# Forming the sums of an output weight by accumulating DRAM transfers instead of on GpSimd, in a fused fp32 encoder layer

## The chip, the cores and the metric

The kernel runs on one core of one Trainium2 chip, as one program. The metric is the device time of one execution in microseconds (us), the median over several executions. The engines named below are TensorE (PE; PEld is its weight load), VectorE (DVE), ScalarE (ACT), GpSimd (POOL) and SyncE (SP). SP and ACT issue plain transfers; in the changed kernel POOL issues transfers too. All matrix products run in fp32 precision by splitting each operand into a rounded high part and a low rest and adding three products (hi·hi, hi·lo, lo·hi).

## The reference

One layer on x of 1024 tokens by 1024 channels, all float32. What the change touches is the product with `w_out` and what follows it:

```python
h = rmsnorm(x, g_mix)
z = h @ w_in                       # pool channels | q | k | v
y_pool = pool_mixer(z[..., :512], w_pool_grp, pool_scale)
y_attn = diff_attention(q, k, v, ...)      # 8 heads, two softmax maps each
gates = sigmoid(h @ w_gate + b_gate)
merged = gates[..., :1024] * (y_pool @ w_branch_pool) + gates[..., 1024:] * (y_attn @ w_branch_attn)
x = x + merged @ w_out             # w_out is 1024 x 1024
h2 = rmsnorm(x, g_ffn)
x = x + square(relu(h2 @ w_up)) @ w_down
```

## The kernel before

The work stands in four stages, in this order.

1. Start and heads (0 to about 690 us of the span). The eight row tiles x0 to x7 (128 tokens each) are loaded, normalised and transposed into hT: x0 to x3 make the first half of hT, x4 to x7 the second. For each row tile, ACT squares it, DVE and POOL make the scale (`rs4` to `rs7`, or `rsa0` to `rsa2` for the first three; the last step is a power on POOL), DVE scales it (`hn4` to `hn7`), PE transposes it into PSUM (`hps`), ACT and DVE split it into hi and lo parts of hT. Then a pipeline runs over 8 heads times 8 row tiles, one step g per head and tile: projection z on PE (stage A), norm of q and k (stage B: `ms` on DVE and POOL, `qn`), transposes, scores, softmax, weighted sum. The gate projection g (`fillers`, weights `fwgate`, raw loads `frgate`) is put in between as filler for PE. `rqkv` are raw loads of a head's weights, `wqkv` their split forms.
2. Branches (about 690 to 800 us). Products with `w_branch_pool` (into `mp`) and `w_branch_attn` (`ba`), gating, merge. In here stands `w_out_sums`, the code that the change removes.
3. Output product (about 800 to 915 us). `merged @ w_out` is computed by a Strassen-Winograd scheme: seven products of half-size blocks, numbered 1 to 7. The sums of activations are made by DVE from the halves of `mp`; the sums of the four blocks of `w_out` were formed earlier and kept in the DRAM tile `w_sum`, from where `w_set` loads them (tiles `ro`, split into `wo`).
4. The MLP, by the same scheme (915 us to the end).

The order on each engine is set by a scheduler that works through the program with priorities; a program's order of writing is a priority and not a place. An instruction that waits for nothing can therefore be put well ahead of where the code has it. The transfers of SP stand in one queue; so do those of POOL, between its other instructions. The sums of `w_out` before, for each of four row blocks d:

```python
for i, b in enumerate((b1, b2)):
    nc.sync.dma_start(b, w_out[(d + 4 * i) * P : (d + 4 * i + 1) * P, :])
(b11, b12), (b21, b22) = ((b[:, 0:512], b[:, 512:D]) for b in (b1, b2))
sub(pool, b11, b12, b11)
sub(pool, b12, b22, b12)
sub(pool, b22, b22, b11)
sub(pool, b21, b21, b22)
for i, b in enumerate((b1, b2)):
    nc.sync.dma_start(w_sum[i][d * P : (d + 1) * P, :], b)
```

The functions that the diff touches:

Of the kernel before, what the change touches and what calls it, by code (L numbers as in the profile page):

```python
# [8 lines left out]
F32 = mybir.dt.float32  # L9
# [3 lines left out]
ALU = mybir.AluOpType  # L13
# [4 lines left out]
P = 128  # L18
S = 1024
D = 1024  # L20
# [23 lines left out]
N_W1, N_W2 = 9, 16  # L44
POOL_W = (3,)
G_DIST, G_COLS = 3, 2

O = "B1 C2 H7 D4 R8 E5 F6 W-2 A0"
ORDER = [(w[0], int(w[1:])) for w in O.split()]
# [14 lines left out]
def encoder_kernel(  # L64
# [21 lines left out]
    nc = tc.nc  # L86
    x, out = x[0], out[0]
    w_in, w_gate, w_out = w_in[0], w_gate[0], w_out[0]
# [4 lines left out]
    dram = ctx.enter_context(tc.tile_pool(name="dram", bufs=1, space=DRAM))  # L93
# [69 lines left out]
    def fu_tile(name):  # L163
        return fq.tile([P, S], F32, tag="fu", name=name)
# [99 lines left out]
    p_dram = dram.tile([POOLD, S], F32, name="p_dram")  # L264
    g_dram = dram.tile([2 * D, S], F32, name="g_dram")
    yd = dram.tile([S, D], F32, name="yd")

    def rsq(dst, ss, n, c):

        nc.vector.tensor_scalar(dst, ss, c, EPS, op0=ALU.mult, op1=ALU.add)  # L270
        nc.gpsimd.tensor_tensor(dst, dst, mhalf[:, :n], op=ALU.pow)  # L271
# [119 lines left out]
    def gates():  # L391
        for c in range(2 * NK - 2):
            yield from gate_cols(c)
        for gen in [gate_cols(c) for c in (2 * NK - 2, 2 * NK - 1)] * 2:
            next(gen)
            yield

    def fillers():
        gate_units = gates()
        for _ in range(G_FIRST):  # L400
            next(gate_units)
            yield
        for g in range(4):
            for _ in pool_group(g):
                yield
                next(gate_units)
                yield
        for _ in gate_units:
            yield
# [3 lines left out]
    with ExitStack() as ph:  # L413
# [35 lines left out]
        def load_x(t):  # L449
            xs[t] = htile([P, D], F32, f"x{t}", 1) if t < 2 else ut([P, D], F32, f"x{t}")  # L450
            for c in range(0, D, 512 if t < 2 else D):
                e = c + 512 if t < 2 else D
                loads[f"x{t}"] = q(nc.sync.dma_start, xs[t][:, c:e], x[t * P : (t + 1) * P, c:e])
# [25 lines left out]
        def split_w(h, kp, eng):  # L479
            rw = raws.pop((h, kp))  # L480
            for i in range(2):
                w = wt([P, 2, 384], f"wqkv{h}_{2 * kp + i}")
                split(w[:, 0, :], w[:, 1, :], rw[:, i, :], eng)
                Wh.setdefault(h, []).append(w)
# [12 lines left out]
        act, dve, pol = nc.scalar, nc.vector, nc.gpsimd  # L497
# [89 lines left out]
        for j in range(2):  # L587
            gb = ps_z.tile([P, 512], F32, tag="z", name=f"gb{j}")
            for i in range(4):
                k = 4 * j + i  # L590
# [301 lines left out]
        def stage(w, g):  # L892
# [19 lines left out]
            elif w == "W" and t == 0 and h:  # L912
                for kp in range(NK // 2):
                    load_w(h, kp)
                    split_w(h, kp, nc.gpsimd)

        units, made = fillers(), 0
        for g in range(-2, N + 10):
            for t in range(4, NT):
                if LX[t] == g:  # L920
                    load_x(t)
            for t in range(1, NT):
                if NX[t] == g:
                    with tc.issue_after(h_hi[t - 2].ins) if t < 6 else nullcontext():
                        norm_x(t)
            if g == G_DIST:
                with behind():
                    distances()
            if g == G_COLS:
                columns()  # L930
            gens = {}
            for tok in ORDER:
                if tok not in gens:
                    i = g - tok[1]
                    gens[tok] = stage(tok[0], i) if 0 <= i < N else iter(())
                next(gens[tok], None)
            for gen in gens.values():
                for _ in gen:
                    pass
            while made < F_UNITS and made < (g - F_FROM) * F_PACE:  # L940
                next(units)
                made += 1
# [4 lines left out]
    def add(eng, out_, a, b):  # L947
        eng.tensor_tensor(out_, a, b, op=ALU.add)

    def sub(eng, out_, a, b):  # L950
        eng.tensor_tensor(out_, a, b, op=ALU.subtract)

    dve, pool = nc.vector, nc.gpsimd

# [4 lines left out]
    def vt(shape, dt, name):  # L959
        return vpool.tile(shape, dt, tag="V", name=name)  # L960
# [22 lines left out]
    ws_bp = {0: load_cols2(w_branch_pool, 0, "bp0")}  # L983
    ypT = [load_split(p_dram, g * P, f"ypT{g}", ypt_tile) for g in range(4)]
    mp, yT, ws_ba = [], [], {}
    w_sum = [dram.tile([S // 2, D], F32, name=f"w_sum{i}") for i in range(2)]

    def w_out_sums(d):

        b1, b2 = (vt([P, D], F32, f"wos{d}_{i}") for i in range(2))  # L990
        for i, b in enumerate((b1, b2)):
            nc.sync.dma_start(b, w_out[(d + 4 * i) * P : (d + 4 * i + 1) * P, :])
        (b11, b12), (b21, b22) = ((b[:, 0:512], b[:, 512:D]) for b in (b1, b2))
        sub(pool, b11, b12, b11)
        sub(pool, b12, b22, b12)
        sub(pool, b22, b22, b11)
        sub(pool, b21, b21, b22)
        for i, b in enumerate((b1, b2)):
            nc.sync.dma_start(w_sum[i][d * P : (d + 1) * P, :], b)

    for d in range(NK):
        if d % 2 == 0 and d + 2 < NK:
            ws_bp[d + 2] = load_cols2(w_branch_pool, (d + 2) * P, f"bp{d + 2}")
        elif d > NK - 4:
            j = len(ws_ba)
            ws_ba[j] = load_cols(w_branch_attn, j * P, f"ba{j}")
        branch_pool(d, ws_bp[d - d % 2][d % 2], bank)
        if d < 4:
            w_out_sums(d)
        if d % 4 < 2:  # L1010
            rb = [fu_tile(f"rb{d}") if d % 2 else ut([P, S], F32, f"rb{d}")]
        else:
            rb = [tmp(f"rb{d}_{i}") for i in range(2)]
        yT.append(load_split(y_dram, d * P, f"yT{d}", yt_tile(d), (rb, r_dram[d])))
    def half(d, th):
        return mp[d][:, th * 512 : (th + 1) * 512]
# [8 lines left out]
    for d in range(NK):  # L1025
        if d + 2 < NK:
            ws_ba[d + 2] = load_cols(w_branch_attn, (d + 2) * P, f"ba{d + 2}")
        ws = ws_ba.pop(d)
        gp = [tmp(f"gp{d}_{th}") for th in range(2)]
        gate([(gp[0], 0, 512), (gp[1], 512, S)], d)  # L1030
        for th in range(2):
            nc.vector.tensor_tensor(half(d, th), half(d, th), gp[th], op=ALU.mult)
        ga = fu_tile(f"ga{d}") if d % 2 else ut([P, S], F32, f"ga{d}")
        gate(whole(ga)[0], NK + d)
        for th in range(2):
            hs = slice(th * 512, (th + 1) * 512)
            ps = proj_T(bank(f"ba{d}_{th}"), ws, lambda k, th: pair(yT[k][th]), th)
            mg = tmp(f"mg{d}_{th}")
            nc.vector.tensor_tensor(mg, ps, ga[:, hs], op=ALU.mult)
            add(pool, half(d, th), mg, half(d, th))  # L1040
            if th == 0:
                a_set("1" if d < 4 else "2", d % 4)
        if d >= 4:
            e = d - 4
            add(dve, half(e, 1), half(e, 1), half(d, 1))
            sub(dve, half(e, 0), half(e, 1), half(e, 0))
            sub(dve, half(d, 0), half(d, 0), half(e, 0))

# [25 lines left out]
    y = {}  # L1076
# [99 lines left out]
    X = [o_bank(f"oX{t}", t) for t in range(4)]  # L1176
# [13 lines left out]
    ws["5"] = w_set("5")  # L1190
    for d in range(4):
        a_set("5", d)
        sub(dve, half(d, 1), half(d + 4, 1), half(d, 0))

    def keep_sum(t, dh):
        k = half(t + 4 * dh, 0)
        xr = tmp(f"xr{t}_{dh}")
        x_rows(xr, 4 + t, dh)
        add(dve, k, X[t], xr)

    for t in range(4):
        o_product(X[t], "6", t, ws["6"])
# [10 lines left out]
    ws["4"] = w_set("4")  # L1213
    for t in range(4):
        o_product(X[t], "3", t, ws["3"])
        add(dve, y[t][:, 512:D], X[t], y[t][:, 512:D])
        nc.sync.dma_start(yd[t * P : (t + 1) * P, :], y[t])
        square(t, 1, y[t][:, 512:D], tmp(f"nsq1_{t}"))
        norm_scale(t, [y[t][:, 0:512], y[t][:, 512:D]])
    Y = {}  # L1220
    for step in O_TAIL.split():
        t = int(step[1])
        if step[0] == "7":
            Y[t] = pb.tile([P, 512], F32, tag="b", name=f"oZ{t}")
            o_product(Y[t], "7", t, ws["7"])
            k = half(t + 4, 0)
            add(dve, k, Y[t], k)
            y_done(k, 4 + t, 1)
            square(4 + t, 1, k, tmp(f"nsq1_{4 + t}"))
        elif step[0] == "a":  # L1230
            for d in range(4):
                a_set("4", d)
        elif step[0] == "n":
            first_half(t)
        elif step[0] == "s":
            second_scale(4 + t)
        elif step[0] == "t":
            second_turn(4 + t, norm_turn(4 + t, lambda j, name: o_bank(name, 2 * (t % 2) + j)))
        else:
            o_product(Y[t], "4", t, ws["4"])  # L1240
            k = half(t, 0)
            add(dve, k, Y[t], k)
            y_done(k, 4 + t, 0)
# [257 lines left out]
    b11 = {}  # L1501
# [117 lines left out]
```

## Time and profile before

| | |
|---|---|
| time, median of 3 executions | 1529.79 us (1528.99 to 1529.82) |
| profiled execution, first to last instruction (span) | 1526.9 us |
| what lies around the span, median less span | 2.9 us |
| PE busy | 1517.4 us of the span |
| DVE, ACT, POOL busy | 1025.5, 794.6, 389.4 us |
| bytes moved by the DMA engines | 213.75 MB, mean 140 GB/s |

The profiled execution's own time is not listed apart from the runs; it is taken as its span and the 2.9 us around it. How to read the views: a row of a group of instructions has line, engine, operation, tiles, count, busy time and mean duration; a row of a wait has who waited, for whom, the total, the number of waits and the longest; a row of a window has its start and end, its length, the busy time of each engine with the count of instructions, the granted TensorE clock, the share of time in which the DMA engines were busy (1.0 is all 16) and the rate. Matmul records can overlap and their ends are modelled, so PE busy says that PE was not waiting, not that it ran at its best rate. Some matmul records can be missing.

### The profile page before, as it was taken

What the parts mean: (1) busy time and instruction counts of PE and PEld (TensorE: products, weight loads), DVE (VectorE), ACT (ScalarE), POOL (GpSimd) and SP (SyncE); (2) the same over time, 40 slices, a digit from 0 to 9 for tenths busy, and PEclk for the clock granted to TensorE, in tenths of its full rate; (3) what the DMA queues carried; (4) which work ended last, traced back from release to release, by engine and by line L of the source; (5) the groups of instructions that cost most, each with busy time, mean ns of one, the idle gap of its engine ahead of it and who ended that gap; (6) DMA issues with size and microseconds to landing.
All of it is one profiled execution on the core that took longest, in us unless ns stands there. A gap on an engine that the chain in (4) does not pass through costs nothing.

```text
span 1526.9 us, 21743 instructions
## 1 busy us (share of the span) xinstructions
PE 1517.4 (99%) x7637; PEld 1316.2 (86%) x7637; DVE 1025.5 (67%) x2135; ACT 794.6 (52%) x1653; POOL 389.4 (26%) x466
## 2 busy tenths in 40 slices
PE   9999999999999999999999999999999999999999
PEld 8899999999999999888888887888888788888887
DVE  7877766677777777742645899676656678556672
ACT  6655555556555555544633467565555634333331
POOL 5525242434334352318646510000000000000000
PEclk9999999999999999999999999999999999999999
DMA  6212111111202021339745633554433899537650
GB/s 213 66 48 66 34 53 52 59 51 39 73 31 80 33 87 49 118 106 376 269 139 174 212 138 117 173 195 156 152 124 111 290 333 367 182 125 260 229 191 28
DMA packets 168583, 213.75 MB, mean 140 GB/s; under 512 B 10165, under 2 KB 104090, under 8 KB 168474
## 3 DMA queue, kind: packets, MB, share of 16 engines
q1 hardware_dynamic: 151050, 185.05, 36.4%
q10 hardware_dynamic: 17424, 27.31, 4.9%
q8 instruction: 60, 0.98, 0.3%
q14 instruction: 49, 0.40, 0.1%
HBM read 154.62 MB, written 57.70 MB: 139 GB/s over the span
## 4 chain that ended last, share of the span: by engine, by line
PE 96%; DVE 2%; DMA 1%; ACT 1%; issue 0%; SPq 0%; POOLq 0%; POOL 0%; ACTq 0%; DVEq 0%
PE z L138 6%; PE z L139 5%; PE z L140 5%; PE Da L139 4%; PE Da L140 4%; PE Da L138 4%; PE g L138 4%; PE g L139 4%; PE g L140 4%; PE Db L138 3%; PE Db L139 3%; PE Db L140 3%; PE X L138 3%; PE X L139 3%; PE X L140 3%; PE sc L767 2%
## 5 line engine op out<-in xcount | busy, mean ns | idle before, releaser
L138 PE MATMUL z<-wqkv,hT 128*128 128x384 f32 x512 | 173.7, 340 | 1.2 <-ACT hT L131 1.1
L140 PE MATMUL z<-wqkv,hT 128*128 128x384 f32 x512 | 173.6, 339 | 0.4 <-DVE hT L437 0.3
L139 PE MATMUL z<-wqkv,hT 128*128 128x384 f32 x512 | 173.2, 338 | 0.0
L778 ACT ACTIVATE s<-s,nm 128x256 f32<-128x256 f32 (+7 forms) x128 | 99.5, 778 | 77.6 <-DVE nm L770 74.3
L271 POOL TENSOR_TENSOR ms<-ms,mhalf 128x4 f32<-128x4 f32 x64 | 66.7, 1042 | 186.8 <-DVE ms L270 183.3
L138 PE MATMUL g<-hT,fwgate 128*128 128x512 f32 x256 | 101.0, 395 | 0.0
L139 PE MATMUL g<-hT,fwgate 128*128 128x512 f32 x256 | 100.5, 392 | 0.0
L140 PE MATMUL g<-hT,fwgate 128*128 128x512 f32 x256 | 100.4, 393 | 0.0
L138 PEld LDWEIGHTS z<-wqkv,hT 128*128 128x128 f32 x512 | 96.2, 188 | 4.0 <-ACT hT L131 1.2
L140 PEld LDWEIGHTS z<-wqkv,hT 128*128 128x128 f32 x512 | 96.2, 188 | 2.6 <-DVE hT L437 0.9
L139 PEld LDWEIGHTS z<-wqkv,hT 128*128 128x128 f32 x512 | 96.3, 188 | 2.4 <-DVE wqkv L437 0.3
L770 DVE CUSTOM_DVE_ANT_0 s<-sc,dist 128x512 f32<-128x512 f32 (+3 forms) x128 | 74.1, 585 | 21.2 <-PE sc L768 20.3
L767 PE MATMUL sc<-K,Q 128*128 128x512 f32 (+2 forms) x192 | 67.5, 357 | 0.4 <-DVE nm L770 0.4
L768 PE MATMUL sc<-K,Q 128*128 128x512 f32 (+2 forms) x192 | 66.1, 349 | 0.0
L132 DVE TENSOR_TENSOR AS<-s,AS 128x512 fp32r<-128x512 f32 x64 | 43.4, 687 | 30.9 <-ACT AS L131 30.9
L132 POOL TENSOR_TENSOR wqkv<-rqkv,wqkv 128x384 fp32r<-128x384 f32 x56 | 58.7, 1065 | 14.6 <-ACT wqkv L131 14.2
L132 POOL TENSOR_TENSOR fwgate<-frgate,fwgate 128x512 fp32r<-128x512 f32 x32 | 43.5, 1361 | 66.0 <-ACT fwgate L131 66.0
L140 PEld LDWEIGHTS g<-hT,fwgate 128*128 128x128 f32 x256 | 48.1, 188 | 9.5
L138 PEld LDWEIGHTS g<-hT,fwgate 128*128 128x128 f32 x256 | 48.1, 188 | 9.1 <-ACT go L387 0.2
L139 PEld LDWEIGHTS g<-hT,fwgate 128*128 128x128 f32 x256 | 48.1, 188 | 8.8
L132 DVE TENSOR_TENSOR AT_0l<-ta,AT_0h 128x512 fp32r<-128x512 f32 (+1 forms) x48 | 32.0, 666 | 32.0 <-ACT AT_0h L131 31.7
L139 PE MATMUL ba<-yT,wba 128*128 128x512 f32 x128 | 49.6, 389 | 0.0
(481 smaller groups left out, 4625.9 us busy)
## 6 DMA issues: line engine op xcount, KB each, us to landing
wd<-in_w_down_dram SPq DMA_DIRECT2D x56, 512.0 KB, 5.4
wu<-in_w_up_dram SPq DMA_DIRECT2D x32, 512.0 KB, 4.3
udS<-us SPq DMA_DIRECT2D x64, 256.0 KB, 3.3
ur<-udS SPq DMA_DIRECT2D x32, 512.0 KB, 4.5
rqkv<-in_w_in_dram SPq DMA_DIRECT2D x64, 192.0 KB, 3.0
ur<-ud SPq DMA_DIRECT2D x24, 512.0 KB, 6.4
frgate<-in_w_gate_dram SPq DMA_DIRECT2D x32, 256.0 KB, 3.6
g_dram<-go ACTq DMA_DIRECT2D x32, 256.0 KB, 3.2
```

Source lines behind the costliest of these rows:

```text
L132: (lo_eng or nc.vector).tensor_tensor(lo, src, f(hi), op=ALU.subtract)
L138: nc.tensor.matmul(ps, lhs_hi, rhs_hi, start=first, stop=False, **kw)
L139: nc.tensor.matmul(ps, lhs_hi, rhs_lo, start=False, stop=False, **kw)
L140: return nc.tensor.matmul(ps, lhs_lo, rhs_hi, start=False, stop=last, **kw)
L271: nc.gpsimd.tensor_tensor(dst, dst, mhalf[:, :n], op=ALU.pow)
L767: nc.tensor.matmul(dst, Q[:, i, 0, :], rhs, start=True, stop=False)
L768: nc.tensor.matmul(dst, Q[:, i, 1, :], rhs, start=False, stop=True)
L770: nc.vector.tensor_tensor_reduce(out=s[i][:, c : c + w], in0=sc[:, 0:w], in1=dist[:, o0 + c : o0 + c + w], scale=2.0 ** -(h + 1), scalar=B ...
L778: nc.scalar.activation(s[i][:, 0:n], s[i][:, 0:n], AF.Exp, bias=last, scale=-1.0, accum_out=Z[:, i, t : t + 1])
```

## The change

The GpSimd sums of stage 2, with their eight loads and eight stores, go. Instead two DRAM tiles are filled by transfers from DRAM to DRAM: four plain copies of a 512x512 block of `w_out` (1.05 MB each) on SP, and seven accumulating transfers of the same size on POOL, each of which adds a block of `w_out` to what lies in `w_sum`. The code calls them from the loop over g, from g = 12 on in steps of 6. Since a transfer can add but not subtract here, all sums become sums with plus signs, and the minus signs move into the sums of activations (`neg_sub`, which is one DVE instruction with a multiply by -1 and a subtract, in 12 places) and into the additions of the products (`sub` for `add`).

```diff
+SUM_FROM, SUM_STEP = 12, 6
...
+    w_sum = [dram.tile([S // 2, D], F32, name=f"w_sum{i}") for i in range(2)]
...
+        def sum_steps():
+
+            q = {f"{i + 1}{j + 1}": w_out[i * 512 : (i + 1) * 512, j * 512 : (j + 1) * 512] for i in range(2) for j in range(2)}
+            s = {f"T{i}": w_sum[n][:, c : c + 512] for i, n, c in ((1, 0, 0), (3, 0, 512), (2, 1, 512), (4, 1, 0))}
+            for dst, src in (("T1", "11"), ("T3", "22"), ("T2", "22"), ("T4", "22")):
+                nc.sync.dma_start(s[dst], q[src])
+            yield
+            for dst, src in (("T1", "12"), ("T3", "12"), ("T2", "12"), ("T4", "12"), ("T2", "11"), ("T4", "11"), ("T4", "21")):
+                nc.gpsimd.dma_start(s[dst], q[src], accum_op=ALU.add)
+                yield
+
         units, made = fillers(), 0
+        sums = sum_steps()
         for g in range(-2, N + 10):
...
+            if g >= SUM_FROM and g % SUM_STEP == 0:
+                next(sums, None)
...
+    def neg_sub(out_, a, b):
+        nc.vector.scalar_tensor_tensor(out_, a, -1.0, b, op0=ALU.mult, op1=ALU.subtract)
...
-    def w_out_sums(d):
...
-        if d < 4:
-            w_out_sums(d)
...
-            add(dve, half(e, 1), half(e, 1), half(d, 1))
-            sub(dve, half(e, 0), half(e, 1), half(e, 0))
-            sub(dve, half(d, 0), half(d, 0), half(e, 0))
+            sub(dve, half(e, 1), half(d, 1), half(e, 1))
+            neg_sub(half(e, 0), half(e, 1), half(e, 0))
+            neg_sub(half(d, 0), half(d, 0), half(e, 0))
...
-        sub(dve, half(d, 1), half(d + 4, 1), half(d, 0))
+        neg_sub(half(d, 1), half(d + 4, 1), half(d, 0))
...
-        add(dve, k, X[t], xr)
+        (sub if dh else add)(dve, k, xr, X[t])
...
-        add(dve, y[t][:, 512:D], X[t], y[t][:, 512:D])
+        sub(dve, y[t][:, 512:D], y[t][:, 512:D], X[t])
...
-            add(dve, k, Y[t], k)
+            sub(dve, k, k, Y[t])
```

The diff doesn't show where the scheduler puts the new transfers. They wait for nothing but each other, and none stands near g = 12 (the second head's middle): all eleven stand within the first head. (T1, T3 are the halves of `w_sum0`, T2 and T4 of `w_sum1`.) Lines of the changed kernel are two higher at the start.

SP, from the first transfer of the program on, before; x0 is the first row tile:

```order
L437 DMA x0_145<-in_x_dram 128x512 x2
L437 DMA rqkv0_0_148<-in_w_in_dram 128x3x128 x2
L437 DMA rqkv0_1_151<-in_w_in_dram 128x3x128 x2
L437 DMA x1_154<-in_x_dram 128x512 x2
L437 DMA rqkv0_2_157<-in_w_in_dram 128x3x128 x2
```

The same place on SP after the change:

```order
L924 DMA w_sum0_130<-in_w_out_dram 512x512
L439 DMA x0_147<-in_x_dram 128x512 x2
L439 DMA rqkv0_0_150<-in_w_in_dram 128x3x128 x2
L439 DMA rqkv0_1_153<-in_w_in_dram 128x3x128 x2
L439 DMA x1_156<-in_x_dram 128x512 x2
```

The first copy has moved ahead of every load of the kernel. Further down on SP, where the second half of the row tiles is loaded, before:

```order
L312 DMA frgate0_1_794<-in_w_gate_dram 128x4x128
L435 DMA rqkv1_0_850<-in_w_in_dram 128x3x128 x2
L435 DMA rqkv1_1_859<-in_w_in_dram 128x3x128 x2
L435 DMA x4_373<-in_x_dram 128x1024
L435 DMA x5_375<-in_x_dram 128x1024
L435 DMA x6_410<-in_x_dram 128x1024
L435 DMA x7_412<-in_x_dram 128x1024
```

And after:

```order
L314 DMA frgate0_1_796<-in_w_gate_dram 128x4x128
L437 DMA rqkv1_0_852<-in_w_in_dram 128x3x128 x2
L924 DMA w_sum0_130<-in_w_out_dram 512x512
L437 DMA rqkv1_1_861<-in_w_in_dram 128x3x128 x2
L924 DMA w_sum1_131<-in_w_out_dram 512x512 x2
L437 DMA x4_375<-in_x_dram 128x1024
L437 DMA x5_377<-in_x_dram 128x1024
L437 DMA x6_412<-in_x_dram 128x1024
L437 DMA x7_414<-in_x_dram 128x1024
```

The other three copies stand just ahead of x4 to x7. POOL, at the end of the second half's norms, before (`ms0_4` belongs to head 0 and row tile 4; `ms` and `qn` are the norm of q and k, `rs7` the scale of x7):

```order
L271 TENSOR_TENSOR rs7_578<-rs7_578,mhalf_102 128x1
L710 TENSOR_TENSOR qn0_3_668<-qn0_3_668,ggh0_377 128x128
L271 TENSOR_TENSOR ms0_4_713<-ms0_4_713,mhalf_102 128x4
L132 TENSOR_TENSOR fwgate2_0_1690<-frgate2_0_1688,fwgate2_0_1690 128x512
L710 TENSOR_TENSOR qn0_4_720<-qn0_4_720,ggh0_377 128x128
```

And after:

```order
L273 TENSOR_TENSOR rs7_580<-rs7_580,mhalf_102 128x1
L133 TENSOR_TENSOR fwgate1_0_1244<-frgate1_0_1242,fwgate1_0_1244 128x512
L133 TENSOR_TENSOR fwgate1_1_1249<-frgate1_1_1247,fwgate1_1_1249 128x512
L927 DMA w_sum1_131<-in_w_out_dram 512x512 x2
L712 TENSOR_TENSOR qn0_3_670<-qn0_3_670,ggh0_379 128x128
L273 TENSOR_TENSOR ms0_4_715<-ms0_4_715,mhalf_102 128x4
L133 TENSOR_TENSOR fwgate2_0_1696<-frgate2_0_1694,fwgate2_0_1696 128x512
L927 DMA w_sum1_131<-in_w_out_dram 512x512
L712 TENSOR_TENSOR qn0_4_722<-qn0_4_722,ggh0_379 128x128
```

Three of the seven accumulating transfers have come in here; each waits for an earlier one into the same half of `w_sum1`. The other four stand further up on POOL: the first ahead of `rsa0`, the scale of x0, the second behind `rs3`, and two behind the split of `fwgate0`, ahead of `ms0_2`. DVE, where the transposes of x4 and x5 are split into hT, before:

```order
L132 TENSOR_TENSOR hT3_1_1_457<-hps4_1_475,hT3_1_0_456 128x2x128
L132 TENSOR_TENSOR hT0_1_1_451<-hps5_0_491,hT0_1_0_450 128x2x128
L132 TENSOR_TENSOR hT2_1_1_455<-hps5_1_501,hT2_1_0_454 128x2x128
L651 COPY cols_121<-cols_ps_510 128x32
L270 TENSOR_SCALAR rs7_578<-ss7_577 128x1
L652 TENSOR_SCALAR gs_122<-cols_121 128x1
L132 TENSOR_TENSOR hT1_1_1_453<-hps5_0_491,hT1_1_0_452 128x2x128
L132 TENSOR_TENSOR hT3_1_1_457<-hps5_1_501,hT3_1_0_456 128x2x128
L282 SCALAR_TENSOR_TENSOR hn7_576<-x7_412,rs7_578,gmb_179 128x512 x2
```

And after:

```order
L133 TENSOR_TENSOR hT0_1_1_453<-hps4_0_467,hT0_1_0_452 128x2x128
L133 TENSOR_TENSOR hT0_1_1_453<-hps5_0_493,hT0_1_0_452 128x2x128
L272 TENSOR_SCALAR rs7_580<-ss7_579 128x1
L284 SCALAR_TENSOR_TENSOR hn7_578<-x7_414,rs7_580,gmb_181 128x512 x2
L133 TENSOR_TENSOR hT1_1_1_455<-hps4_0_467,hT1_1_0_454 128x2x128
```

Before, x4 and x5 were split in full ahead of `hn7`, the scaling of x7; after, `hn7` stands ahead of three quarters of that split.

More of the change, by code (lines that the diff above doesn't have):

```diff
@@ L985, in encoder_kernel @@
     mp, yT, ws_ba = [], [], {}
-    w_sum = [dram.tile([S // 2, D], F32, name=f"w_sum{i}") for i in range(2)]
-    def w_out_sums(d):
[L990 to L999, printed above, removed]
     for d in range(NK):
```

## The prediction, as it was put on record

> **What bounds the kernel now.** I read the page's span, busy times and chain first, then windows by stage, then what PE waited for, and last the start in order of time.
>
> ```profile
> span 1526.9 us, 21743 instructions
> PE 1517.4 (99%) x7637; PEld 1316.2 (86%) x7637; DVE 1025.5 (67%) x2135; ACT 794.6 (52%) x1653; POOL 389.4 (26%) x466
> PE 96%; DVE 2%; DMA 1%; ACT 1%; issue 0%; SPq 0%; POOLq 0%; POOL 0%; ACTq 0%; DVEq 0%
> ...
> 2.00:26.00 24.00, 23.23 (x133) 19.95 (x132) 19.08 (x50) 16.22 (x42) 8.65 (x13) 1.00 0.94 303
> 26.00:40.00 14.00, 12.90 (x73) 11.32 (x72) 11.90 (x22) 7.82 (x20) 10.03 (x11) 1.00 0.27 77
> 40.00:60.00 20.00, 20.00 (x117) 18.66 (x118) 15.83 (x48) 13.66 (x40) 6.67 (x12) 1.00 0.11 38
> 60.00:690.00 630.00, 629.55 (x3627) 578.80 (x3626) 445.55 (x1326) 356.42 (x906) 234.33 (x317) 1.00 0.20 63
> 690.00:740.00 50.00, 50.00 (x222) 41.40 (x221) 19.91 (x20) 23.32 (x42) 40.61 (x30) 1.00 1.04 387
> 740.00:915.00 175.00, 175.00 (x802) 145.38 (x801) 119.28 (x172) 85.95 (x166) 85.69 (x63) 1.00 0.52 171
> 915.00:1526.90 611.90, 605.85 (x2671) 499.85 (x2669) 393.96 (x502) 290.59 (x441) 1.96 (x1) 1.00 0.55 189
> ```
>
> A window row gives start and end, length, then busy PE, PEld, DVE, ACT, POOL, clock, DMA share, GB/s. PE is the bound nearly everywhere: 1526.9 less 1517.4 leaves 9.5 us in which it had nothing to do, and the clock is 1.00 throughout. Those 9.5 us lie at the start (0.8 + 1.1, and 1.1 ahead of the first matmul), in the heads (0.45) and behind 915 us (6.1). From 690 to 915 us, where the sums are made and used, PE is busy 225.00 of 225 us. The number of PE instructions does not change, so the time can only move by PE waiting less or more.
>
> What the change removes, by tile, and who waits for PE or by it from 60 to 915 us:
>
> ```profile
> L992 SPq DMA_DIRECT2D wos<-in_w_out_dram x8: 328/432/837, 689.1 to 713.3; - x8
> L951 POOL TENSOR_TENSOR wos<-wos x8: 1282/1287/2275, 697.0 to 728.2; 128x512 f32<-128x512 f32 x8
> L951 POOL TENSOR_TENSOR wos<-wos,wos x8: 1277/1286/1757, 699.9 to 724.4; 128x512 f32<-128x512 f32 x8
> L193 SPq DMA_DIRECT2D ro<-w_sum x8: 360/377/386, 819.5 to 866.8; - x8
> ...
> PE sc L767 <- DVE nm L770: 0.4, 1, 0.4
> ```
>
> The sixteen GpSimd sums are done at about 730 us and first loaded at 819.5, 90 us later. PE's only wait between 60 and 915 us is 0.4 us, in the heads. So the work that goes has a price of nothing today.
>
> The start is another matter. In order of time, from SP, ACT, PE, POOL and the chain:
>
> ```profile
> 0.74 0.85 SPq L437 DMA_DIRECT2D x<-in_x_dram  x2
> 3.49 0.63 ACT L437 ACTIVATE hn<-x 128x512 f32<-128x512 f32 x1 [0.86 <-DMA x<-in_x_dram]
> 5.35 0.55 POOL L437 TENSOR_TENSOR rsa<-rsa,mhalf 128x1 f32<-128x1 f32 x1 [3.23 <-DVE rsa L437]
> 7.85 1.03 PE L437 MATMUL hps<-identf,hn 128*128 128x128 f32 x8
> 16.70 2.14 SPq L435 DMA_DIRECT2D x<-in_x_dram  x4
> 17.71 8.00 DMA x<-in_x_dram
> ...
> 22.00:24.00 2.00, 1.99 (x14) 1.91 (x14) 2.00 (x6) 0.57 (x2) 1.45 (x1) 1.00 1.01 395
> 24.00:26.00 2.00, 2.00 (x13) 1.86 (x11) 1.23 (x5) 2.00 (x6) 0.72 (x2) 1.00 0.67 274
> 26.00:28.00 2.00, 2.00 (x13) 2.00 (x13) 1.67 (x1) 1.06 (x3) 2.00 (x3) 1.00 0.03 12
> ```
>
> From 2 to 26 us the sixteen DMA engines are full (0.94, 303 GB/s). The transfers of x4 to x7, issued at 16.70 to 18.84, land up to 25.7, and then the engines are empty (0.03). So loads wait their turn behind what was issued before them, and the start is bound by the DMA queue, with PE just behind it.
>
> **The change, part by part.** *Removed: nothing gained.* Sixteen sums of 1.29 us, 20.6 us of POOL, and 8.4 MB of transfers leave a window in which PE never waited. Cover: PE's 50.00 of 50. Their absence also empties the DMA queue there (1.04), again for no wait of PE.
>
> *Twelve sums of two operands become `neg_sub`; the other sums keep their kind.* The rows are
>
> ```profile
> L951 DVE TENSOR_TENSOR mp<-mp,mp 128x512 f32<-128x512 f32 x8 | 8.6, 1082 | 0.1
> L1128 DVE SCALAR_TENSOR_TENSOR y<-y,nrs,gfb 128x512 f32<-128x512 f32 x8 | 5.6, 747 | 1.2 <-DMA yd<-y 1.1
> ```
>
> The form used now takes no longer than the one before (747 against 1082, beside busier POOL). Even 0.2 us more each, 2.4 us, is covered: DVE is busy 119 of 175 us there and PE waits for none of it. I take 0; if that cover went, 2.4.
>
> *First copy, ahead of x0.* It is 512 x 512 x 4 bytes, 1.05 MB. At the start's 303 GB/s it takes 3.5 us, at the 387 of the 690 to 740 window 2.7. Up to 7.85 PE ran only warm-up products and then took the transposes of x0 without a gap, so x0 landing later is PE idle, one for one. POOL's `rsa0` now also stands behind the first accumulating transfer, which itself waits for this copy; copy and x0 land close together, so I add nothing for that. This 3.5 us is not added to the next part: both shift the same row, the first matmul of z for x4, and the later shift is the one that lasts.
>
> *Three copies ahead of x4 to x7.* The start moves 24 us x 303 GB/s = 7.3 MB until x7 has landed. The four copies are 4.19 MB more in the same queue: 13.8 us at 303, 10.8 at 387, and 27.7 if a byte that is read from and written to DRAM costs an engine twice what a load costs. No transfer from DRAM to DRAM is in this trace. I take 13.8, since the 387 of the 690 window is a mixture of reads and writes and still a full rate.
>
> *Accumulating transfers into T1 and T3.* They start when their copy has landed, on POOL's own queue, and use the same engines: 2.1 MB, 0 us if they only fill gaps (there are none: 0.94), 6.9 at one pass, 13.8 at two. I take 6.9. x7 then lands at 25.7 + 13.8 + 6.9 = 46.4 us.
>
> From x7 to z:
>
> ```profile
> 40.28 1.08 ACT L278 ACTIVATE hn<-x 128x1024 f32<-128x1024 f32 x1
> 41.48 0.15 DVE L270 TENSOR_SCALAR rs<-ss 128x1 f32<-128x1 f32 x1 [0.41 <-ACT hn L278]
> 41.78 0.56 POOL L271 TENSOR_TENSOR rs<-rs,mhalf 128x1 f32<-128x1 f32 x1 [0.73 <-DVE gs L652]
> 42.42 1.40 DVE L282 SCALAR_TENSOR_TENSOR hn<-x,rs,gmb 128x512 f32<-128x512 f32 x2
> 43.74 0.41 DVE L132 TENSOR_TENSOR hT<-hps,hT 128x256 fp32r<-128x256 f32 x1
> 40.00 0.41 PE L138 MATMUL z<-wqkv,hT 128*128 128x384 f32 x1 [1.08 <-ACT hT L131]
> ...
> 40.76 0.17 PE z L138
> ```
>
> These are the steps of x7, the first matmul of z for x4, which even now waited 1.08 us, and one of z's matmuls on the chain (0.17). Before, z could start ahead of `hn7`; in the new order of DVE, `hn7` stands ahead of most of the split that z reads. From 40.28 to 43.74 + 0.41 are 3.9 us; PE can do six matmuls of z (6 x 0.17 = 1.0 us) meanwhile. So z starts, in effect, at 46.4 + 2.9 = 49.3 instead of 40.0: 9.3 us that PE loses for good.
>
> *Accumulating transfers into T2 and T4* start when copies 3 and 4 have landed, beside x4 to x7: 2.1 MB, between 0 and 6.9 us of x7's landing. I take half, 3.5.
>
> The Trainium skill, DMA: Bandwidth & Descriptors, Queues, rings and completion order, says that a DMA engine takes one queue's descriptors in order and goes round-robin between queues that have work. The rows above agree with the first half; by the second, all four accumulating transfers would take their full turn, 3.5 us more, and the time below would be 1547.5. The same page, Latency and other measured facts, gives 207 to 214 GB/s for copies between tensors in HBM; by 214 the four copies take 19.6 us, an estimate, and the time would be 1549.8. No run here shows either yet.
>
> *POOL's waits.* The second transfers into T2 and T4, and then the third into T4, wait for the one before them; behind them on POOL stand `qn0_3`, `ms0_4` and then `qn0_4`, `ms0_5`. PE needs `qn0_3` some 10 us after z starts, about when an accumulating transfer of 7 to 10 us is done. 0 to 5 us; I take 1.5. The issue itself has no row on POOL; the nearest are 0.43 us on SP and 1.29 us for a POOL sum, within the 1.5.
>
> Sum: 9.3 + 3.5 + 1.5 = 14.3 us of new PE idle. Against the profiled execution: 1526.9 + 14.3 = 1541.2, and 2.9 us around the span (median 1529.79 less 1526.9) give 1544 us.
>
> **The rivals.**
>
> 1. *The start hides it (not slower).* The slack is there: z starts at 40.0 and x7 needs 2.9 us, so x7 could land 11.4 us later than 25.7 at no cost. If copies run at 387 GB/s or better and accumulating transfers only fill gaps, x7 lands at 36.5 and only the first copy's 2.7 us at x0 remain: 1532.5. It decides where copies cost no more than 2.9 us each and the rest yields. For it: 395 GB/s in the window from 22 us; against it: 0.94 share over 24 us.
>
> 2. *GpSimd becomes the wait.* If making and waiting for each accumulating transfer holds POOL for 5 us and more, `rsa0`, `ms0_1`, `ms0_2`, `qn0_3` and `ms0_5` are all late, each a step that PE's next product needs: five holds of 3 to 4 us on top, about 16 us, or 1560. For it: one queue, with POOL's short steps on PE's path at 5.35. Against it: POOL is busy only 8.65 of 24 us there.
>
> 3. *The order on the chip is another one,* and the transfers run from g = 12 on, where the DMA share is 0.20: no cost, 1530. The program's order speaks against it.
>
> **How the numbers follow.** 0.2% of this time, 3.1 us, is about what a measurement can tell. Forecast 0.70 (4 to 24 us slower), GpSimd 0.15, hidden 0.12, other order 0.03. Slower is forecast and GpSimd, 0.85; of the other 0.15, 0.02 goes to faster for small luck in the 6.1 us behind 915, and 0.13 to same. The low end is rival 1's 1532; the high end takes copies at twice the cost, 27.7 for 13.8, 1544 + 13.9 = 1558, which leaves out half of rival 2.
>
> **What would show it.** Right: PE idle ahead of the transposes of x0 (3 us) and ahead of z for x4 (near 50 us), x7's square on ACT past 45 us, DMA share near 1 until then; 690 to 740 us with a lower DMA share and PE still full; PE busy unchanged near 1517. Wrong: z for x4 near 43 us (copies cheap), or POOL standing at the accumulating transfers with PE waiting for `ms` or `qn` after 55 us.

## The result and the profile after

The changed kernel takes 1558.2 us, median of 4 executions (1556.8 to 1559.2), against 1529.8 for the kernel before on the same chip: 1.0183 times, 95% interval 1.0169 to 1.0198. The forecast was 1544, so the direction and the place were as said, and the size was half of what came: 28.4 us for 14.3. The value stands at the very end of the range, which went up to 1558. Line numbers after are up to 3 higher than before (the z products are L139 to L141, the start's instructions L439).

The page of the changed kernel: span, busy times, PE and its clock by slices (40 slices of 38.9 us), and the two queues that the change touches.

```profile
span 1555.7 us, 21699 instructions
PE 1527.8 (98%) x7637; PEld 1325.1 (85%) x7637; DVE 1015.3 (65%) x2135; ACT 794.8 (51%) x1653; POOL 371.5 (24%) x457
PE   7799999999999999999999999999999999999999
PEclk8799999999999999999999999999999999999999
...
q1 hardware_dynamic: 150858, 180.86, 35.3%
q0 software_dynamic: 3696, 7.34, 2.8%
```

The number of PE instructions is the same. PE is idle for 27.9 us (1555.7 less 1527.8), 18.4 more than before, and busy for 10.4 us more. The last row is POOL's queue with the seven accumulating transfers: 2.8% of 1555.7 us are 43.6 us of all sixteen DMA engines, 6.2 us for each.

Stage by stage, with the columns of the windows before (length, busy PE, PEld, DVE, ACT, POOL, granted clock, DMA share, GB/s):

```profile
2.00:26.00 24.00, 15.27 (x70) 13.83 (x70) 9.57 (x23) 8.70 (x21) 3.87 (x6) 0.77 0.96 250
26.00:40.00 14.00, 13.42 (x73) 12.04 (x72) 9.91 (x30) 8.01 (x22) 6.84 (x10) 0.91 0.96 299
40.00:60.00 20.00, 14.53 (x69) 12.13 (x67) 8.11 (x21) 7.15 (x16) 10.04 (x13) 0.83 1.10 261
60.00:80.00 20.00, 14.92 (x68) 12.96 (x69) 9.06 (x26) 9.16 (x25) 7.42 (x7) 0.74 0.80 145
80.00:100.00 20.00, 19.82 (x112) 18.46 (x111) 14.46 (x47) 11.29 (x36) 10.48 (x15) 1.00 0.74 154
100.00:690.00 590.00, 589.55 (x3419) 544.04 (x3418) 425.66 (x1280) 338.56 (x866) 220.00 (x302) 1.00 0.19 59
690.00:720.00 30.00, 30.00 (x150) 25.22 (x149) 9.26 (x24) 13.03 (x24) 7.17 (x6) 1.00 0.44 145
```

Nearly all of it lies ahead of 80 us. From 2 to 80 us PE is idle for 19.9 us (before: 1.9), its mean clock in each row is below 1, and the DMA engines, which before stood at 0.27 and 0.11 from 26 to 60 us, are full up to 60 us and at 0.74 or more, in the mean of a row, up to 100. They are not full all along; one shorter window:

```profile
65.00:70.00 5.00, 4.58 (x15) 3.48 (x15) 2.06 (x8) 2.46 (x6) 3.02 (x4) 0.50 0.25 67
```

The gate weights are loaded into a few tiles, and SP issues the next load only when GpSimd has split an earlier one; up to 100 us it waits 29.5 us for these splits, so in this stretch the loads wait for other engines and not for the queue. From 100 us on PE is as full as it was.

What PE waited for, longest first, and ACT in order of time with its idle time and what ended it:

```profile
PE hps L439 <- ACT hn L439: 6.0, 1, 6.0
PE z L139 <- ACT hT L132: 5.8, 2, 5.4
PE hps L289 <- ACT dist L647: 3.5, 1, 3.5
PE z L139 <- ACT wqkv L439: 2.8, 1, 2.8
```

```profile
9.72 0.63 ACT L439 ACTIVATE hn<-x 128x512 f32<-128x512 f32 x1 [7.08 <-DMA x<-in_x_dram]
...
47.72 1.06 ACT L280 ACTIVATE hn<-x 128x1024 f32<-128x1024 f32 x1 [5.88 <-DMA x<-in_x_dram]
...
57.40 1.06 ACT L280 ACTIVATE hn<-x 128x1024 f32<-128x1024 f32 x1 [0.53 <-PE hps L289]
...
63.72 0.62 ACT L132 CAST fwgate<-frgate 128x512 fp32r<-128x512 f32 x1 [5.17 <-DMA frgate<-in_w_gate_dram]
64.24 0.64 ACT L132 CAST hT<-hps 128x256 fp32r<-128x256 f32 x2
```

x0 is squared at 9.72 instead of 3.49, x4 at 47.72 instead of 24.32, x7 at 57.40 instead of 40.28. The cast of hT that z of x4 needs stands on ACT behind the cast of the second gate's weights, which waited 5.17 us for its load; z then goes on at 64.66:

```profile
64.66 0.69 PE L139 MATMUL z<-wqkv,hT 128*128 128x384 f32 x1 [5.41 <-ACT hT L132]
```

### The profile page after: what moved, and what is told of

It reads as the page before. It is cut to its first block, busy times and chain, and to the rows that moved or that the text cites. A ratio compares the mean times of both kernels' runs of the same rounds, so it can differ in the third digit from the quotient of the medians.

```text
span 1555.7 us, 21699 instructions
## 1 busy us (share of the span) xinstructions
PE 1527.8 (98%) x7637; PEld 1325.1 (85%) x7637; DVE 1015.3 (65%) x2135; ACT 794.8 (51%) x1653; POOL 371.5 (24%) x457
## 3 DMA queue, kind: packets, MB, share of 16 engines
q0 software_dynamic: 3696, 7.34, 2.8%
## 4 chain that ended last, share of the span: by engine, by line
PE 89%; DMA 5%; DVE 4%; POOL 1%; issue 1%; ACT 1%; POOLq 0%; SPq 0%; ACTq 0%; DVEq 0%
PE z L139 5%; PE z L140 5%; PE z L141 5%; PE Da L140 4%; PE Da L141 4%; PE Da L139 4%; PE g L141 4%; PE g L140 4%; PE g L139 4%; PE Db L139 3%; PE Db L140 3%; PE Db L141 3%; PE X L139 3%; PE X L141 3%; PE X L140 3%; PE sc L769 2%
## 5 line engine op out<-in xcount | busy, mean ns | idle before, releaser
L139 PE MATMUL z<-wqkv,hT 128*128 128x384 f32 x512 | 177.8, 347 | 9.1 <-ACT hT L132 5.8
L141 PE MATMUL z<-wqkv,hT 128*128 128x384 f32 x512 | 176.6, 345 | 0.1
L140 PE MATMUL z<-wqkv,hT 128*128 128x384 f32 x512 | 176.0, 344 | 0.0
L139 PEld LDWEIGHTS z<-wqkv,hT 128*128 128x128 f32 x512 | 98.6, 192 | 13.2 <-ACT hT L132 6.8
L139 PE MATMUL g<-hT,fwgate 128*128 128x512 f32 x256 | 100.8, 394 | 0.0
L141 PE MATMUL g<-hT,fwgate 128*128 128x512 f32 x256 | 100.4, 393 | 0.0
L140 PEld LDWEIGHTS z<-wqkv,hT 128*128 128x128 f32 x512 | 98.6, 193 | 2.1 <-DVE wqkv L439 0.3
L141 PEld LDWEIGHTS z<-wqkv,hT 128*128 128x128 f32 x512 | 98.3, 192 | 2.0 <-DVE hT L437 0.6
L141 PEld LDWEIGHTS g<-hT,fwgate 128*128 128x128 f32 x256 | 48.1, 188 | 9.5
L139 PEld LDWEIGHTS g<-hT,fwgate 128*128 128x128 f32 x256 | 48.1, 188 | 9.0 <-ACT go L389 0.2
```

Source lines behind the costliest of these rows:

```text
L139: nc.tensor.matmul(ps, lhs_hi, rhs_hi, start=first, stop=False, **kw)
L140: nc.tensor.matmul(ps, lhs_hi, rhs_lo, start=False, stop=False, **kw)
L141: return nc.tensor.matmul(ps, lhs_lo, rhs_hi, start=False, stop=last, **kw)
```

## The experiments

Twelve kernels were run, each beside runs of the kernel before. Times are medians; ratios are to the kernel before, with a 95% interval.

| kernel | us | ratio |
|---|---|---|
| signs alone | 1530.1 | 1.0001 (0.9992 to 1.0010) |
| sums left out | 1529.4 | 0.9997 (0.9988 to 1.0007) |
| whole change, late | 1532.3 | 1.0013 (1.0005 to 1.0022) |
| late copies alone | 1529.4 | 0.9997 (0.9988 to 1.0006) |
| copies alone, early | 1540.0 | 1.0066 (1.0052 to 1.0079) |
| plain for accumulating | 1552.3 | 1.0143 (1.0126 to 1.0160) |
| copies 2 to 4 behind x7 | 1551.5 | 1.0139 (1.0124 to 1.0154) |
| first copy behind x3 | 1559.1 | 1.0185 (1.0169 to 1.0200) |
| all copies behind x7 | 1552.8 | 1.0148 (1.0134 to 1.0162) |
| gate casts held | 1559.6 | 1.0187 (1.0172 to 1.0202) |
| start filled | 1558.2 | 1.0186 (1.0172 to 1.0200) |
| kernel before, no warm-up | 1530.0 | 1.0002 (0.9993 to 1.0011) |

### What the change removes, and its signs

The kernel before without the sums; the four products that used them read plain blocks of `w_out`:

```diff
-        if d < 4:
-            w_out_sums(d)
-"6": (w_sum[1], 0, 1), "5": (w_sum[0], 0, 0), ... "7": (w_sum[0], 0, 1), "4": (w_sum[1], 0, 0)
+"6": (w_out, 0, 1), "5": (w_out, 0, 0), ... "7": (w_out, 0, 1), "4": (w_out, 4, 0)
```

> The kernel before without any sums of the output weight: no GpSimd sums, no loads and stores for them; products 4 to 7 read plain blocks of w_out in their place, so this leaves out that part of the computation. It is the ceiling of what the removal can bring. Theory A (PE never waited there): 1529.8, within 1.5 us. Rival D (the removal brings something the early cost hides): 1527 or less.

The signs alone, with GpSimd's sums kept:

```diff
-        sub(pool, b11, b12, b11)   # and the three others
+        add(pool, b11, b12, b11)
# activation sums as in the changed kernel; sum_steps() left out
```

> Only the signs: the sums of the output weight are made by GpSimd as before, with plus signs, and the activation sums and additions have the changed signs. Theory A: 1529.8, within 1.5 us of the kernel before. Rival C: 2 us or more slower, with PE waiting between 770 and 945 us.

Both are the kernel before. The window of the kernel without sums:

```profile
690.00:740.00 50.00, 50.00 (x222) 41.42 (x221) 20.45 (x26) 29.20 (x51) 20.70 (x15) 1.00 0.74 242
```

POOL drops from 40.61 to 20.70 us and the DMA share from 1.04 to 0.74, and PE is full in both. The most that the change could have won is nothing.

### The same transfers elsewhere

```diff
-SUM_FROM, SUM_STEP = 12, 6
+SUM_FROM, SUM_STEP = 30, 5
+                with tc.issue_after(latest["sp"].ins):      # a head's weight load
                     nc.sync.dma_start(s[dst], q[src])
+                with tc.issue_after(latest["pool"].ins):    # a power on POOL
                     nc.gpsimd.dma_start(s[dst], q[src], accum_op=ALU.add)
```

> The whole change, with the copies held on SP behind the weight loads of head 4 and the seven accumulating transfers on POOL behind norm steps from head 4 on. Theory A (all of the 28 us comes from the transfers standing in the start, where the DMA engines were full): 1529 to 1532 us, no PE idle over 1 us between 60 and 690 us, since the DMA share there was 0.20. Rival B (accumulating transfers cost wherever they stand, by holding GpSimd or by slowing loads): 1537 us or more, PE waiting for ms or qn near each of them. Rival C (signs and what comes behind cost): over 1532 with PE waits behind 690 us.

With the copies issued at 302 us and the accumulating transfers between 334 and 625 us, 26 of the 28.4 us are gone: where the transfers run is what costs. 2.4 us stay, just above what A allowed (1532). PE's waits and the first of the seven issues on POOL:

```profile
PE z L140 <- POOL wqkv L133: 1.1, 3, 0.6
```

```profile
333.85 1.27 POOL L931 DMA_DIRECT2D w_sum<-in_w_out_dram  x1
```

The same without the seven accumulating transfers (T1 to T4 stay plain copies):

```diff
-                with tc.issue_after(latest["pool"].ins):
-                    nc.gpsimd.dma_start(s[dst], q[src], accum_op=ALU.add)
                 yield
```

> The kernel with the whole change made late (copies near 302 us), without its seven accumulating transfers on GpSimd. Theory A (the 2.4 us that the late version still cost come from those seven issues, 1.1 to 1.3 us each on GpSimd, which delay its splits of wqkv): 1529.5 to 1530.5, and PE's waits for GpSimd's wqkv (1.1 us in the late version) are gone. Rival B (the rest is from the copies' 14 us of DMA engines near 302 us, or from the scheduler's order around them): 1531.5 to 1532.5.

1529.4: the rest was the accumulating transfers, and three waits of PE for POOL's splits of `wqkv` (1.1 us) go with them. The profiled execution of the late version took 1531.0 us, 1.3 less than the median, so this profile has no row for the rest. These quiet places also give clean prices. The window around the copies, of the kernel before and then of this one:

```profile
296.00:330.00 34.00, 34.00 (x194) 31.24 (x193) 25.14 (x73) 20.95 (x50) 17.72 (x21) 1.00 0.25 75
```

```profile
296.00:330.00 34.00, 34.00 (x194) 31.33 (x193) 25.41 (x73) 21.02 (x52) 17.99 (x22) 1.00 0.68 202
```

Four copies are 0.43 of 34 us, 14.6 us of all DMA engines, 3.7 each. One accumulating transfer alone, before and in the late version:

```profile
330.00:350.00 20.00, 20.00 (x117) 18.54 (x116) 15.24 (x44) 10.42 (x24) 4.98 (x9) 1.00 0.06 21
```

```profile
330.00:350.00 20.00, 20.00 (x117) 18.54 (x116) 15.43 (x44) 10.52 (x25) 6.62 (x10) 1.00 0.46 73
```

0.40 of 20 us, 8.0 us for the same bytes as one copy. The next one by itself, from 380 to 400 us, comes to 6.4 us (0.63 less 0.31), and the row of POOL's queue gives 3.1% of 1529.2 us for the seven, 6.8 each.

### Which transfers cost, in the changed kernel's place

Copies alone, with the seven accumulating transfers left out:

```diff
-                nc.gpsimd.dma_start(s[dst], q[src], accum_op=ALU.add)
```

> The changed kernel with the four early copies and without the seven accumulating transfers, which leaves the sums out. Theory A with the prediction's price (3.5 us a copy at 303 GB/s): x7 lands near 40 us and the time is 1538 to 1542. If the copies are nearly all of the cost: 1552 or more. If the accumulating transfers are: 1533 to 1536, the 6 us at x0 alone.

1540.0: the copies cost 10.2 us, the accumulating transfers the other 18.1. PE's waits and ACT's square of x4:

```profile
PE hps L439 <- ACT hn L439: 4.3, 1, 4.3
PE z L141 <- DVE hT L133: 2.9, 1, 2.9
```

```profile
37.77 1.06 ACT L280 ACTIVATE hn<-x 128x1024 f32<-128x1024 f32 x1 [5.52 <-DMA x<-in_x_dram]
```

Plain transfers on POOL's queue instead (the sums are left out):

```diff
-                nc.gpsimd.dma_start(s[dst], q[src], accum_op=ALU.add)
+                nc.gpsimd.dma_start(s[dst], q[src])
```

> The whole change, but the seven transfers on GpSimd's queue copy instead of accumulating: same bytes, same issues, same waits, the sums are left out. Theory A (an accumulating byte costs the DMA engines about twice what a copied one does: 43.6 us of all 16 engines for 7.34 MB, 6.2 us a transfer): plain, each takes 3 to 3.5 us, so of the 18.1 us between the kernel with copies alone (1540.0) and the changed one (1558.2) about half goes: 1545 to 1551, and GpSimd's queue shows 20 to 26 us of engine time. Rival B (the cost is the second queue's turn, the bytes and GpSimd's waits, not the accumulating): 1555 to 1560, engine time near 43 us.

1552.3 lies between the two ranges, nearer to A's end (1551) than to B's (1555); the engine time decides for A on the accumulating itself. POOL's queue and x4:

```profile
q0 software_dynamic: 1904, 7.34, 1.5%
```

```profile
47.05 1.06 ACT L280 ACTIVATE hn<-x 128x1024 f32<-128x1024 f32 x1 [9.65 <-DMA x<-in_x_dram]
```

1.5% of 1549.9 us are 23.2 us, 3.3 for each transfer, so the accumulating doubles the engines' time (43.6). That doubling is worth 5.9 of the 18.1 us. The larger part, 12 us, comes with seven more megabyte transfers on a queue that need not wait behind SyncE's: x4's square is 9.3 us later than with copies alone, although x4 stands in the other queue. (2.7 of these are a later issue of x4's load, at 28.49 us instead of 25.82.) GpSimd also stands 17.1 us at these transfers, waiting for earlier ones to land; what of the 12 us that makes is not separated here. The Trainium skill, DMA: Bandwidth & Descriptors, Queues, rings and completion order, has the engines serve queues in turn; this trace agrees.

### Does the order of the copies matter?

Copies two to four behind x4 to x7:

```diff
+                with tc.issue_after(loads["x7"].ins) if dst != "T1" else nullcontext():
                     nc.sync.dma_start(s[dst], q[src])
```

> The first copy and its place ahead of x0 stay; copies two to four go behind the loads of x4 to x7 on SyncE's queue, and the accumulating transfers with them (T1's first one depends on the first copy alone and still runs from about 9.4 us). Theory A (delays at x0 and at x4 add up, each paid in PE idle and again at half clock): the wait ahead of the transposes of x0 stays 4 to 6 us, the one ahead of z for x4 goes under 1 us: 1535 to 1541. Rival B (the prediction's rule: a shift at x0 is contained in the later one, so alone it costs what the copy moves x0, 3.5 us, and nothing more): 1532 to 1534.5.

The first copy behind x3:

```diff
+                with tc.issue_after(loads["x3"].ins):
                     nc.sync.dma_start(s[dst], q[src])
```

> The opposite part: the first copy goes behind x3's load, so that x0 lands as before, and all four copies with their accumulating transfers stay ahead of x4 to x7. Theory A (the two delays add up): PE waits nothing ahead of the transposes of x0, 8 to 13 us around z for x4 (45 to 70 us), clock halved after it: 1544 to 1551, and this kernel's cost and that of the one before add up to about 28 us. Rival B (only the later shift lasts): PE waits as much at z of x4 as it did in both places together, 1554 to 1559.

All four behind x7:

```diff
+                with tc.issue_after(loads["x7"].ins):
                     nc.sync.dma_start(s[dst], q[src])
```

> All four copies go behind the loads of x4 to x7 on SyncE's queue, the accumulating transfers behind them as before, so that x0 to x7 land as in the kernel before; behind the copies stand the weight loads of the second gate and of head 1. Theory A (what counts is that any load which PE wants within the next 50 us is late, whichever it is): x4's square on ScalarE stays near 25 us, but a cast of frgate waits for its load and PE with it: 1540 to 1552. Rival B (the prediction's picture: the cost is x0's and x4's lateness alone): 1530 to 1533.

Both theories failed for the first (1551.5). For the second, the time is B's within 0.1 us (1559.1): x0 is on time (ACT squares it at 3.41), no wait is left ahead of its transposes, and the whole is not faster by it. PE waits later instead:

```profile
PE hps L289 <- DVE hn L284: 7.2, 1, 7.2
PE z L141 <- DVE hT L439: 6.7, 2, 6.5
```

But only the first of these is B's, the late x4. The second stands at 26.53 us, where x0 to x3 are on time, and comes from GpSimd: it stood 9.66 us at the first accumulating transfer until its copy had landed, with the norm step `ms` behind it. DVE waited for that step, and z behind DVE:

```profile
23.32 1.28 POOL L928 DMA_DIRECT2D w_sum<-in_w_out_dram  x1 [9.66 <-DMA w_sum<-in_w_out_dram]
25.72 0.42 DVE L706 TENSOR_TENSOR qn<-z,ms 128x256 f32<-128x256 f32 x1 [7.02 <-POOL ms L273]
```

So a wait at GpSimd took the place of the one at x0, and what the first copy costs by itself is not shown by this run.

The third is the telling one: 1552.8, slightly above A's range and nowhere near B's. All of x is on time, and the weights of the second gate are not:

```profile
25.19 1.06 ACT L280 ACTIVATE hn<-x 128x1024 f32<-128x1024 f32 x1 [0.39 <-DMA x<-in_x_dram]
56.60 0.62 ACT L132 CAST fwgate<-frgate 128x512 fp32r<-128x512 f32 x1 [10.28 <-DMA frgate<-in_w_gate_dram]
63.92 0.62 ACT L132 CAST fwgate<-frgate 128x512 fp32r<-128x512 f32 x1 [6.43 <-DMA frgate<-in_w_gate_dram]
```

```profile
58.09 1.09 PE L289 MATMUL hps<-identf,hn 128*128 128x128 f32 x4 [8.49 <-DVE hT L133]
65.41 1.09 PE L289 MATMUL hps<-identf,hn 128*128 128x128 f32 x4 [6.23 <-DVE hT L133]
```

Most of the same cost comes by another load. GpSimd has a part in it here too. It stood 5.96 us at its first accumulating transfer, so that the split of the first gate's weights came at 34.03 us (before: 26.27), and SP issued the next gate loads behind that split at 35.72 instead of 27.58. Of the 23.4 us by which the first cast above is late (56.60 instead of 33.19), 8.1 are this later issue. One product waited for the split itself:

```profile
33.11 1.27 POOL L928 DMA_DIRECT2D w_sum<-in_w_out_dram  x1 [5.96 <-DMA w_sum<-in_w_out_dram]
PE g L141 <- POOL fwgate L133: 3.4, 1, 3.4
```

The transfers in question are 14.6 + 43.6 = 58 us of all engines; put in front of x or behind it, within the first 100 us they make some load or some step of GpSimd late that PE wants, for 21 to 29 us.

### One link of the new chain

No transfer moves; ScalarE's casts of the second gate's weights go behind those of x7's transposes:

```diff
+            with tc.issue_after(h_hi[7].ins) if name == "gate1" else nullcontext():
                 split(w[:, 0], w[:, 1], rw, nc.gpsimd)
```

> The whole change, with ScalarE's two casts of the second gate's weights held behind the last cast of x7's transposes; no transfer moves. Theory A (z of x4 waited for a weight load of the gates: its casts stand on ScalarE behind the cast of frgate, whose load took 25.3 us in the DMA queue): the 5.4 us wait of z at 64.66 us shrinks to under 1.5 us and some of the half-clock stretch after it goes: 1548 to 1554. Rival B (the cast is late but not the last: x5 to x7 and their transposes, landing up to 57 us, would hold PE in its place): 1556 to 1559, with the wait moved to transposes or z of x5.

1559.6, slightly above B's range and far from A's. The 5.4 us wait of z went, and one of the same size came not at the transposes or z of x5, as B had it, but at another in-order step of ACT, the casts of Q for the first scores, which now stood behind a cast of `fwgate` that waited for `frgate`:

```profile
PE sc L771 <- ACT Q L743: 5.9, 1, 5.9
```

So the row that the chain of waits shows (z behind the gate's cast) is how the late load reaches PE here, and not what it costs.

### The clock

The changed kernel with PE's first idle stretch filled, and the kernel before without warm-up products:

```diff
-N_W1, N_W2 = 9, 16
+N_W1, N_W2 = 9, 72        # changed kernel
-N_W1, N_W2 = 9, 16
+N_W1, N_W2 = 0, 0         # kernel before
```

> The changed kernel with 56 more warm-up products ahead of the transposes of x0 (72 for 16), which fill PE's idle stretch from 7.3 to 13.2 us; nothing else moves. Theory A (PE's clock is halved by that idle stretch, so the transposes and first products of z run at half speed from 12 to 18 us): the clock there stays at 1.00, PE's first products of z are done by 16.5 us instead of 18.9; but the next wait (a weight cast at 21.4 us) takes most of it, so the whole gains 0 to 3 us: 1555 to 1558. Rival B (the half clock is tied to the busy DMA engines and not to idleness): the clock stays at 0.50 from 12 to 18 us with the fill, and the time at 1558 to 1562, if the fill overshoots.

> The kernel before with none of the 25 warm-up products at its start; every load is on time. Theory A (PE idle up to the transposes of x0 at 7.85 us leaves the clock at half for some us): the profile shows 0.50 from about 6 to 13 us, and the time grows by half of that stretch, 2 to 4 us: 1532 to 1534, with DMA and all else as before. Rival B (a half clock at the start costs nothing, since loads and casts bound there): 1529.5 to 1530.5.

One window of the changed kernel, and the same of the filled one:

```profile
12.00:18.00 6.00, 4.77 (x18) 4.76 (x19) 4.80 (x11) 3.89 (x10) 1.44 (x2) 0.50 1.03 160
```

```profile
12.00:18.00 6.00, 5.97 (x44) 5.38 (x42) 3.86 (x8) 3.80 (x10) 1.03 (x2) 1.00 1.03 164
```

At the same DMA share the clock is 1.00 where PE was kept busy and 0.50 where it had stood for 6 us: it follows PE's idleness (A). The Trainium skill, TensorE: Matmul & The Clock Gate, Part 1, says the same, and the trace agrees. The time does not move (1558.2), but this run can't say what the half clock costs, since more than the fill came out different. The transposes of x0 start at 14.69 us instead of 13.23, and the second accumulating transfer stands further ahead on GpSimd, which waits there for its copy, with `ms` behind it as above:

```profile
35.73 1.06 POOL L927 DMA_DIRECT2D w_sum<-in_w_out_dram  x1 [15.99 <-DMA w_sum<-in_w_out_dram]
PE z L141 <- DVE hT L439: 8.2, 2, 7.9
```

Without warm-up, in the kernel before, B holds (1530.0); two rows of it:

```profile
9.21 0.52 PE L139 MATMUL z<-wqkv,hT 128*128 128x384 f32 x1
13.45 0.33 PE L138 MATMUL z<-wqkv,hT 128*128 128x384 f32 x1
```

z's products take 0.52 us until 13 us and 0.33 after it, and this costs nothing. (The window of the same kernel, next, has its clock column at 1.00 all the while.)

```profile
8.00:12.00 4.00, 4.00 (x16) 3.99 (x15) 3.02 (x10) 3.57 (x10) 1.01 (x1) 1.00 1.12 339
```

So in the kernel before a half clock at the start is free. That the 10.4 us more of "busy" in the changed kernel are waiting in another form, as there, is likely but not shown, and what the 0.74 of 60 to 80 us costs was not tried by itself.

## Why the prediction was right in kind and half in size

That the time lies within the range is in part luck: its upper end came from copies at twice their cost, 27.7 us, and the copies took 14.6. The cost came from elsewhere.

- *Removed sums: 0.* Right, shown by leaving them out. *Signs: 0.* Right.
- *First copy, contained in the later shift.* Too small for x0 itself: 6.2 us (9.72 less 3.49), not 3.5. That it costs nothing of its own stays open: with x0 on time the whole gains nothing, but there a wait at GpSimd had come in its place.
- *Four copies, 13.8 us of the queue.* Right: 14.6, which is 287 GB/s for 4.19 MB. The Trainium skill, DMA: Bandwidth & Descriptors, Latency and other measured facts, gives its 207 to 214 GB/s for copies of tiles of 128 rows of 16 KiB at certain distances between the rows; the rate measured here decides, and the estimate of 19.6 us was too long.
- *Accumulating transfers, 3.5 us each at one pass.* Mis-sized: 6.2 us each in the changed kernel, 6.8 in the late version. This is worth 5.9 us of the 18.1 that the seven cost.
- *x7's landing sets the end.* This step failed. The sum counted the two accumulating transfers ahead of x4, half of the next two, nothing of the last three but POOL's wait, and stopped at x7 and z: x7 was to land at 46.4 us and z of x4 to start, in effect, at 49.3. In the changed kernel ACT squares x6 just behind its landing, at 53.16, and x7 comes after x6 on the queue; z of x4 starts at 56.97, stops after six products and goes on at 64.66:

```profile
53.16 1.06 ACT L280 ACTIVATE hn<-x 128x1024 f32<-128x1024 f32 x1 [1.10 <-DMA x<-in_x_dram]
56.97 0.67 PE L139 MATMUL z<-wqkv,hT 128*128 128x384 f32 x1
```

  The loads behind x7 on the same queue, the gate weights, were never in it. With all of x on time the kernel is still 23.0 us slower. The working should have gone on until the DMA engines are empty again. One more window of the kernel before:

```profile
60.00:80.00 20.00, 20.00 (x122) 19.01 (x120) 16.29 (x42) 12.48 (x35) 13.19 (x16) 1.00 0.35 102
```

  With 0.27 and 0.11 from 26 to 60 us the engines had 14 x 0.73 + 20 x 0.89 + 20 x 0.65 = 41 us free up to 80 us, for 58 us of new work that PE's loads have to share.
- *POOL's waits: 1.5.* Apart from the issues themselves, GpSimd stands at four of the seven until an earlier transfer has landed, 19.5 us in all:

```profile
POOL w_sum L927: 19.5, 4
```

  In the changed kernel no wait of PE over 0.4 us stands directly behind one of these, so GpSimd as the bound (rival 2), though it names nearly the time, is not what the rows show there. The split of the gate weights at 39.10 us, which lets SP issue the late gate loads, stands behind the transfer at 35.91 and may be late by some 2 us for it (an estimate from GpSimd's rows from 35.91 to 39.10). But the link that rival 2 names is real. In three variants, where the scheduler gave the transfers other places on GpSimd, it made PE wait 6.5 us (first copy behind x3), 3.4 (all copies behind x7) and 7.9 (start filled). No kernel kept the transfers in the start and moved them behind GpSimd's other work, so its share of the 28.4 us is not separated. In the late version, where PE is full, the accumulating transfers cost 2.4 us.
- *PE busy unchanged near 1517.* Wrong: 1527.8, with the clock at half for part of the first 80 us.

Open stays how the 28.4 us divide between the single late loads and GpSimd's stops: each that was put right in these runs handed its wait to another.

## What to carry to other kernels

A transfer that nothing waits for is not free: at a start that is bound by the DMA queue it delayed the loads behind it, and on a second queue those beside it too. An accumulating transfer that must follow another also stops what stands behind it on its issuing engine until the other has landed. Price it by the engines' time until they are empty again, go through all loads in that stretch and not only the next one, and first ask what the removed work could win: here PE never waited for it. If such transfers are wanted, hold them by an explicit order to a stretch with a low DMA share; written later in the program is not later on the queue.

## What was not expected of the hardware

An accumulating DRAM transfer costs the DMA engines twice what a plain one does (43.6 us against 23.2 for 7.34 MB), and its issue holds GpSimd for 1.0 to 1.4 us. PE's clock was at 0.50 after 6.0 us of idling (at 13.23 us) and again after 2.8 us (at 22.00), and z's products took 0.52 us instead of 0.34 for the next 4.7 and 6.2 us of work, so "busy" grows with no more work done. And the clock column shows 1.00 from 8 to 12 us of the kernel without warm-up, where the products themselves take 0.52 us instead of 0.33: here the durations show the half speed and the column does not.
